# One hybrid layer on one core: preloaded banks 0 to 2, copies out inside the last step, and pauses ahead of transposes

## The chip, the cores and the metric

The kernel runs on one core of one Trainium2 chip. The metric is the device time of one execution in microseconds (us). TensorE (PE) multiplies, VectorE (DVE), ScalarE (ACT) and GpSimd (POOL) work on tiles, SyncE (SP) issues most of the transfers.

## The reference: what is computed

One layer over 256 latent tokens `x` and 256 context tokens `ctx` of width 4096, in float32. A modulation is computed from two vectors, normalised rows are scaled and shifted by it, projected by a 4096 x 13312 matrix, mixed in three ways, and projected back:

```python
mod_l = silu(c) @ w_ada + b_ada          # 4096 -> 3 * 4096, the same for c_ctx
hl = rmsnorm(xl, norm_g) * (1.0 + sc_l) + sh_l
hc = rmsnorm(xc, norm_g) * (1.0 + sc_c) + sh_c
z_l, z_c = hl @ w_in, hc @ w_in          # split into conv (3), recurrence (2), attention q k v and gate (4)
ya = conformer_conv(...)                 # GLU, depthwise conv over 31, LayerNorm, pointwise
yb = sum of two RG-LRU scans, started from the context's last state
yc = 8x16 neighbourhood attention over the latent grid, plus attention to the context
mix = concat(ya * silu(a_gate), yb * silu(r_gate), yc * silu(c_gate))
out = rmsnorm(xl + g_l * (mix @ w_out), final_g)
```

Only the latent stream is returned, so of the context's projections only r_x, k and v are needed.

## The kernel before

**Phases.** Weights are float32 and every product is made of three: a weight tile is split into a high part `hi` (ACT, L411) and a low part `lo` (DVE, L417), the activations likewise, and PE multiplies hi by hi, hi by low, low by hi (L426, all inside `Step.products`). A *chunk* is 512 columns of a weight matrix. In the first phase both token streams are multiplied by the columns for r, k and v, in 10 chunks of `w_in`: r0, k0, v0, k1, v1, k2, v2, k3, r1, v3 (`kinds`, L861). An r or k chunk ("both") fills 4 PSUM banks of 128 x 512, a v chunk ("tm") 2. The second phase does the remaining columns for the latent tokens alone, with the mixers' work on the other engines, and ends with `w_out`.

**Blocks.** The 32 row tiles of `w_in` come in 13 blocks of 1, 1, 2, 2, 2 and then 3 rows (`BLOCKS`), because the modulation for a row has to be there before its activations h can be made. So each of the 10 chunks is visited 13 times, and its sums live in SBUF tiles `acc` between the visits. At the start of a visit some banks are *preloaded* with the sums so far (ACT copy, L859) and the matmuls add to them; at its end the bank is copied back out (*spilled*, ACT copy, L848). A bank that isn't preloaded starts at zero, and DVE adds it to `acc` (L853). Before the change banks 1, 2, 3 of an r or k chunk and bank 1 of a v chunk are preloaded (`ch.pre`, L875). `spill` and `preload` of all banks are called one after the other at the end of a chunk's last step (L1232 to L1237). The banks of the chunks come from a pool of five (tag "g", L80); three more serve everything else (tag "aux", counted by `take` and `give`).

**Steps and order.** A step is up to two rows of a chunk, so a block of three rows has steps of two and one, and the last step of a chunk is its tail. The program order is written out by the generator: `do_step` emits, in rounds of three products (one bank, one row), the products of a step, and between rounds the work of threads (`run_threads`). A thread is a Python generator; `yield None` waits for the next round. Threads of rank 0 (the end of a modulation, the making of h) go ahead at every round, others only while the planner's budget for DVE and ACT allows. `ahead.split_high()` and `split_low()` in a step make the parts for the step after next; `load_until` issues transfers four steps ahead into six buffers.

**Modulation.** `MODS` lists groups of rows with a flag: part 0 (scale) is always multiplied on PE (`mod_matmuls`, L268, into a bank `psa`), part 1 (shift) on PE or, with flag 1, on DVE (L921, L923, into the tile `gboth`). `spread` deals the pieces over the steps so that each group is done by its due time, which lies half the preceding block's planned time ahead of the block that uses it (L892). The end of a group is a thread: `mod_finish` copies `psa` to SBUF (DVE, L273), transposes it on PE (L280), sums (DVE, L283) and adds (L260, L262); `mod_finish_vector` transposes `gboth` (L297) for each of two streams and sums (L299). Then `next_h` makes h (DVE L362, ACT L363, DVE L370), and a block's first chunk calls `drain` on it, which runs the thread to its end.

**Recurrence.** From the last block on, two threads run `recurrence` for eight heads each, with two matmuls per head (L533, L534).

Of the kernel before, what the change touches and what calls it, by code (L numbers as in the profile page):

```python
# [17 lines left out]
P = 128  # L18
# [7 lines left out]

BLOCKS = [1, 1, 2, 2, 2, 3, 3, 3, 3, 3, 3, 3, 3]

MODS = [(1, 1, 0), (2, 2, 0), (4, 2, 0), (6, 2, 0), (8, 4, 0), (12, 4, 0), (16, 4, 1), (20, 4, 1), (24, 4, 1),
        (28, 4, 1)]  # L30

NPG, NWD, NRAW, NHI = 69, 6, 6, 3
# [11 lines left out]
def tile_hybrid_layer(ctx: ExitStack, tc: tile.TileContext, x, c, cctx_tok, c_ctx, w_ada, b_ada,  # L44
# [89 lines left out]
    def drain(*ths):  # L134

        for _ in range(2000):
            if all(t.done for t in ths):
                return
            for t in list(threads):
                if not t.done and (t in ths or t.rank == 0 or clock["aux"] > 0):  # L140
                    advance(t, True)
            clock["tick"] += 1
        raise RuntimeError("a thread waits for ever")

    def take(n):

# [7 lines left out]
    with tc.manual_schedule():  # L154
# [116 lines left out]
        def mod_finish(part, k0, s, ps):  # L271

            V.tensor_copy(adas[:, :s * P], ps[:, :s * P])  # L273
            give(1)
            yield 0.6 * s / 4 + .1, 0
            yield None
            yield from take(1)
            pm = bank("psm")
            for i in range(s):
                tr(pm[:, i * P:(i + 1) * P], adas[:, i * P:(i + 1) * P], ident)  # L280
            yield None
            sums = small(8, "sums").rearrange("p (k o) -> p k o", o=2)
            V.reduce_sum(sums[:, :s], pm[:, :s * P].rearrange("p (k q o) -> p k o q", q=4, o=32)[:, :, 0:2], axis=AX.X)  # L283
            mod_columns(part, k0, s, sums)
            give(1)
            yield 0.5, 0

        def mod_finish_vector(k0, s):
            sums = small(8, "sums").rearrange("p (k o) -> p k o", o=2)
            yield None  # L290
            yield None
            for b in range(2):
                yield None
                yield from take(1)
                pm = bank("psm")
                for i in range(s):
                    tr(pm[:, i * P:(i + 1) * P], gboth[:, b, i * P:(i + 1) * P], ident)  # L297
                yield None
                V.reduce_sum(sums[:, :s, b:b + 1], pm[:, :s * P].rearrange("p (k n) -> p k n", n=P), axis=AX.X)  # L299
                give(1)  # L300
                yield 0.7, 0
            mod_columns(1, k0, s, sums)
            yield 0.2, 0
# [78 lines left out]
        acc = {}  # L382
# [115 lines left out]
        def recurrence(d):  # L498
# [12 lines left out]
            for n in range(8):  # L511
                while n > rec_done[1 - d] + 1:
                    yield None
                Xr = acc[("r", n // 4), n % 4]
                x3 = Xr.rearrange("p (s t) -> p s t", s=2)
                gw = rec[2 + n % 2][:, d]
                G.dma_start(gw[:, 0], w_r[0, d, n])
                G.dma_start(gw[:, 1], w_i[0, d, n])
                ci = 8 * d + n
                A.activation(xc, Xr, AF.Identity, scale=tap(3 if d == 0 else 0), bias=col("rcb", ci))  # L520
                yield 0, 0.7
                yield None
                for s in (1, 2, 3):
                    if d == 0:
                        o, i_, w = xc3[:, :, s:], x3[:, :, :T - s], tap(3 - s)
                    else:
                        o, i_, w = xc3[:, :, :T - s], x3[:, :, s:], tap(s)
                    V.scalar_tensor_tensor(o, i_, w, o, ALU.mult, ALU.add)
                    yield 0.75, 0
                yield None  # L530
                yield from take(2)
                pr, pi = bank("pr"), bank("pi")
                mm(pr, gw[:, 0], xc, start=True, stop=True)  # L533
                mm(pi, gw[:, 1], xc, start=True, stop=True)  # L534
                yield None
                yield None
                A.activation(ti, pi, AF.Tanh, bias=hbi[:, ci:ci + 1], scale=0.5)
                give(1)

                A.activation(e, pr, AF.Relu, bias=nbr[:, ci:ci + 1], scale=-1.0)  # L540
                yield 0, 1.4
                A.activation(pr, pr, AF.Tanh, bias=hbr[:, ci:ci + 1], scale=0.5)
                A.activation(e, e, AF.Exp, scale=-1.0)
                yield 0, 1.4
                A.activation(pr, pr, AF.Abs)
                yield 0, 0.6
                yield None
                V.scalar_tensor_tensor(ti, ti, 1.0, xc, ALU.add, ALU.mult)
                V.scalar_tensor_tensor(e, pr, 1.0, e, ALU.add, ALU.mult)
                yield 1.4, 0  # L550
                yield None
                A.activation(xc, e, AF.Exp, scale=n4[:, ci:ci + 1])
                A.activation(e, e, AF.Tanh, scale=p4[:, ci:ci + 1])
                yield 0, 1.4
                A.activation(pr, xc, AF.Square)
                yield 0, 0.6
                yield None
                V.scalar_tensor_tensor(e, pr, 1.0, e, ALU.add, ALU.mult)
                give(1)
                yield 0.7, 0  # L560
                yield None
                A.activation(e, e, AF.Sqrt, bias=tiny)
                yield 0, 3.2
                yield None
                V.scalar_tensor_tensor(ti, e, 0.5, ti, ALU.mult, ALU.mult)
                yield 0.7, 0
                if d == 0:
                    V.tensor_tensor_scan(e[:, :T], xc[:, :T], ti[:, :T], 0.0, ALU.mult, ALU.add)
                    V.tensor_tensor_scan(hold[:, n % 2], xc[:, T:], ti[:, T:], e[:, T - 1:T], ALU.mult, ALU.add)
                    yield 1.5, 0  # L570
                else:
                    for s, init in ((0, 0.0), (1, e[:, 0:1])):
                        sl = slice(s * T, s * T + T)
                        V.tensor_tensor_scan(e[:, sl][:, ::-1], xc[:, sl][:, ::-1], ti[:, sl][:, ::-1], init,
                                             ALU.mult, ALU.add)
                    yield 1.5, 0
                    while rec_done[0] <= n:
                        yield None
                    V.tensor_add(ybs(n), hold[:, n % 2], e[:, T:])
                    yield 0.4, 0  # L580
                rec_done[d] += 1
# [259 lines left out]
            unpair(sil)  # L841


        def spill(ch, key):

            for i, b in enumerate(ch.banks):
                if i in ch.pre:
                    A.copy(acc[key, i], b)  # L848
                elif (key, i) not in acc:
                    acc[key, i] = page([P, 512], name="acc")  # L850
                    (A.copy if i % 2 else V.tensor_copy)(acc[key, i], b)
                else:
                    V.tensor_add(acc[key, i], acc[key, i], b)  # L853

        def preload(ch, key):
            for i in range(ch.nb):
                ch.banks[i] = bank("g" + ch.kind, "g")
                if i in ch.pre:
                    A.copy(ch.banks[i], acc[key, i])  # L859

        kinds = [("r", 0), ("k", 0), ("v", 0), ("k", 1), ("v", 1), ("k", 2), ("v", 2), ("k", 3), ("r", 1), ("v", 3)]  # L861
        starts = [sum(BLOCKS[:i]) for i in range(len(BLOCKS))]
# [1 line left out]
        begin = {}  # L864
        t = 0.0
        for bi, s in enumerate(BLOCKS):
# [3 lines left out]
            for ci, key in enumerate(order):  # L870
# [1 line left out]
                c0 = {"r": C_RX, "k": C_K, "v": C_V}[kind] + 512 * i  # L872
                ch = Chunk(key, win, ks, c0, "tm" if kind == "v" else "both", ctx_ops if kind == "v" else None)
                if bi:
                    ch.pre = {1} if kind == "v" else {1, 2, 3}  # L875
                    ch.before = lambda ch=ch, key=key: preload(ch, key)
                ch.after = lambda ch=ch, key=key: spill(ch, key)
                ch.block, ch.place = bi, ci
                for st in ch.steps():
                    st.at = t  # L880
# [5 lines left out]
        class Mod:  # L886
            def __init__(self, part, k0, s, vec):
# [1 line left out]
                self.thread = None  # L889
                self.held = []  # L890
                bi = max(i for i in range(len(BLOCKS)) if starts[i] <= k0)
                self.due = begin[bi] - (0.5 * (begin[bi] - begin[bi - 1]))  # L892
                self.n = 2 if s > 2 else 8 // s

            def items(self):
# [293 lines left out]
        def do_step(i):  # L1189
# [23 lines left out]
            if tail:  # L1213
                clock["v"] -= PAGE * (ch.nb - len(ch.pre))
                clock["a"] -= PAGE * (1.7 * len(ch.pre) if ch.block else 1)
            if ahead:
                ahead.split_high()
            work = st.mods + st.vecs
            n = len(st.kp)
            for p in range(ch.nb * n):  # L1220
# [8 lines left out]
                clock["tick"] += 1  # L1229
                if p == n - 1 and ahead:  # L1230
                    ahead.split_low()
            if tail:  # L1232
                if ch.after is not None:
                    ch.after()
                nxt = steps[i + 1].ch if i + 1 < len(steps) else None
                if nxt is not None and nxt.before is not None:
                    nxt.before()  # L1237
                if ch.block == len(BLOCKS) - 1 and ch.place == 1:
                    rec_threads.extend(spawn(recurrence(d), 2) for d in range(2))
            if ch in chunks3 and i + 1 < len(steps) and head:  # L1240
# [92 lines left out]
```

## Time and profile before

| | |
|---|---|
| median of 3 runs | 2430.76 us (2427.84 to 2431.7) |
| the profiled execution | 2434.84 us |
| its span, first to last instruction | 2433.1 us |
| PE, DVE, ACT busy | 95%, 66%, 52% of the span |
| read from HBM | 544.58 MB |

PE is 0.9 busy or more in most of the 40 slices of the page; the first phase takes the first 1008 us. A matmul's end is modelled, so a busy PE is not always multiplying at its full rate, and the distance of two starts tells more than the duration.

### The profile page before, as it was taken

The page shows a single profiled execution, that of the slowest core. Times are in us where ns is not written, and L with a number is a line of the kernel's source. Part 1 is how long each engine was busy: PE and PEld are TensorE (multiplying, and loading weights), DVE is VectorE, ACT ScalarE, POOL GpSimd, SP SyncE. Part 2 cuts the span into 40 slices and gives each one's busy share as a digit, 9 for nine tenths or more (in the row PEclk, how much of TensorE's full clock was granted, in tenths as well). Part 3 has the DMA queues.
Part 4 walks back from the last instruction along what each step waited for, and adds up shares of the span by engine and source line. Part 5 has one row for each costly group of instructions (what it writes and reads, how often), then busy time and mean ns, then how long its engine had stood idle before and what let it go on. Part 6 is the DMA issues. An engine that isn't in the chain of part 4 may idle for free.

```text
span 2433.1 us, 29898 instructions
## 1 busy us (share of the span) xinstructions
PE 2301.2 (95%) x10761; PEld 1753.7 (72%) x10761; DVE 1594.2 (66%) x2196; ACT 1271.5 (52%) x1860; POOL 96.0 (4%) x133
## 2 busy tenths in 40 slices
PE   6999889899989999999999999999999999999997
PEld 4555556676666776777768888788888778888886
DVE  4543446676766543667667798788967677667655
ACT  4665444455545666777776444444444444444433
POOL 0000000000000000000100100110011021000000
PEclk8999999999999999999999999999999999999999
DMA  9988788767767543555557888878878678887864
GB/s 278 288 262 265 270 273 290 246 220 239 259 208 246 182 121 91 157 157 169 159 162 222 228 280 263 202 242 260 261 204 231 189 217 293 266 265 251 262 213 164
DMA packets 293484, 550.76 MB, mean 226 GB/s; under 512 B 19199, under 2 KB 60887, under 8 KB 293335
## 3 DMA queue, kind: packets, MB, share of 16 engines
q1 hardware_dynamic: 287904, 536.94, 68.5%
q0 software_dynamic: 4480, 11.54, 4.2%
q8 instruction: 84, 1.38, 0.2%
q14 instruction: 65, 0.53, 0.1%
q10 hardware_dynamic: 951, 0.37, 0.1%
HBM read 544.58 MB, written 4.19 MB: 226 GB/s over the span
## 4 chain that ended last, share of the span: by engine, by line
PE 71%; ACT 3%; DVE 3%; issue 2%; DMA 1%; POOL 0%; SPq 0%; ACTq 0%; DVEq 0%; POOLq 0%
PE gtm L426 50%; PE gboth L426 13%; PE y L682 1%; ACT hi L411 1%; PE sc L642 1%; DMA raw<-in_w_in_dram 1%; PE gcm L426 1%; PE psa L268 1%; ACT acc L848 1%; DVE lo L417 1%; PE pr L533 1%; PE pi L534 1%; PE pt L667 1%; PE turn L602 0%; DVE gboth L923 0%
## 5 line engine op out<-in xcount | busy, mean ns | idle before, releaser
L417 DVE TENSOR_TENSOR lo<-raw,hi 128x1024 fp32r<-128x1024 f32 (+1 forms) x660 | 756.7, 1149 | 624.9 <-ACT hi L411 596.5
L411 ACT CAST hi<-raw 128x1024 fp32r<-128x1024 f32 (+1 forms) x660 | 648.5, 986 | 725.5 <-PE gtm L426 420.9
L426 PE MATMUL gtm<-hi,lh 128*128 128x512 f32 x2560 | 835.6, 401 | 1.0 <-ACT hi L411 1.0
L426 PEld LDWEIGHTS gtm<-hi,lh 128*128 128x128 f32 x2560 | 482.6, 189 | 112.0 <-issue 11.2
L426 PE MATMUL gboth<-h,hi 128*128 128x512 f32 x1536 | 505.8, 411 | 47.8 <-ACT acc L848 43.0
L426 PE MATMUL gtm<-lo,lh 128*128 128x512 f32 x1280 | 501.5, 392 | 7.2 <-DVE lo L417 7.2
L426 PEld LDWEIGHTS gboth<-h,hi 128*128 128x128 f32 x1536 | 281.6, 192 | 179.5 <-ACT acc L848 69.4
L426 PE MATMUL gboth<-h,lo 128*128 128x512 f32 x768 | 305.4, 398 | 0.0
L426 PE MATMUL gtm<-hi,mix 128*128 128x512 f32 x976 | 304.0, 391 | 0.0
L426 PEld LDWEIGHTS gtm<-lo,lh 128*128 128x128 f32 x1280 | 241.6, 189 | 69.3 <-DVE lo L417 11.4
L426 PEld LDWEIGHTS gtm<-hi,mix 128*128 128x128 f32 x976 | 183.7, 188 | 37.8
L426 PE MATMUL gtm<-lo,mix 128*128 128x512 f32 x488 | 190.4, 390 | 0.2 <-DVE lo L417 0.2
L848 ACT COPY acc<-gboth 128x512 f32<-128x512 f32 x216 | 125.0, 586 | 123.3 <-PE gboth L426 113.0
L426 PE MATMUL gtm<-hi,h 128*128 128x512 f32 x512 | 182.6, 408 | 3.9 <-DVE acc L853 2.2
L426 PEld LDWEIGHTS gboth<-h,lo 128*128 128x128 f32 x768 | 147.4, 192 | 34.0 <-DVE lo L417 0.3
L923 DVE SCALAR_TENSOR_TENSOR gboth<-raw,scol,gboth 128x512 f32<-128x512 f32 x248 | 169.6, 747 | 0.0
L1123 DVE SCALAR_TENSOR_TENSOR gboth<-raw,scol,gboth 128x1024 f32<-128x1024 f32 x124 | 160.1, 1292 | 0.0
L426 PEld LDWEIGHTS gtm<-hi,h 128*128 128x128 f32 x512 | 96.8, 189 | 54.7 <-issue 22.1
L859 ACT COPY gboth<-acc 128x512 f32<-128x512 f32 x216 | 117.6, 594 | 0.0
L268 PE MATMUL psa<-raw,cpad 128*32 128x512 f32 (+2 forms) x1152 | 112.6, 469 | 1.1 <-DMA raw<-in_w_ada_dram 0.6
L426 PEld LDWEIGHTS gtm<-lo,mix 128*128 128x128 f32 x488 | 91.9, 188 | 19.6 <-DVE lo L417 0.8
L426 PE MATMUL gtm<-lo,h 128*128 128x512 f32 x256 | 101.0, 395 | 0.1
(228 smaller groups left out, 1650.1 us busy)
## 6 DMA issues: line engine op xcount, KB each, us to landing
raw<-in_w_in_dram SPq DMA_DIRECT2D x430, 512.0 KB, 4.4
raw<-in_w_ada_dram SPq DMA_DIRECT2D x384, 512.0 KB, 4.7
raw<-in_w_out_dram SPq DMA_DIRECT2D x128, 512.0 KB, 4.6
raw<-in_w_in_dram SPq DMA_DIRECT2D x100, 256.0 KB, 4.2
xp<-in_ctx_dram SPq DMA_DIRECT2D x16, 256.0 KB, 6.9
xp<-in_x_dram SPq DMA_DIRECT2D x16, 256.0 KB, 6.6
xr<-in_x_dram POOLq DMA_DIRECT2D x16, 256.0 KB, 4.6
raw<-in_w_pw_dram SPq DMA_DIRECT2D x8, 512.0 KB, 7.7
```

The costliest lines, as they stand in the source:

```text
L268: mm(ps[32 * q:32 * q + 32, :W], cpad[(k + j) // 16][:, (k + j) % 16, :], raw[:, j, :], start=(k + j < 4), stop=(k + j >= KT - 4))
L411: A.copy(self.hi[:, :n], self.raw[:, :n])
L417: V.tensor_sub(self.lo[:, :n], self.raw[:, :n], self.hi[:, :n].bitcast(F32))
L426: one = lambda o, l, r, start, stop: mm(o, l, r, start=start, stop=stop, skip_group_check=True)
L533: mm(pr, gw[:, 0], xc, start=True, stop=True)
L534: mm(pi, gw[:, 1], xc, start=True, stop=True)
L642: mm(ps, q[i][:, qt * P:(qt + 1) * P], acc[("k", g), i], start=True, stop=True)
L667: tr(ps[:, kt * T + qt * P:kt * T + qt * P + P], Ps[0][qt][:, (2 * kp + kt) * P:(2 * kp + kt + 1) * P], ident)
L848: A.copy(acc[key, i], b)
L859: A.copy(ch.banks[i], acc[key, i])
L923: V.scalar_tensor_tensor(a, self.raw[:, j], s, a, ALU.mult, ALU.add)
L1123: V.scalar_tensor_tensor(a, self.raw, s, a, ALU.mult, ALU.add)
```

## The change

Five things. Banks 0, 1 and 2 (0 of a v chunk) are preloaded instead of 1, 2, 3 (1). The preloads of the next chunk are emitted ahead of the tail's products (bank 0, and bank 1 too where the chunk is a v) and behind each bank's copy out, and each bank is copied out right behind its last products. Pauses of six rounds stand ahead of the transposes of modulation sums, and of two rounds ahead of the recurrence's matmuls; the vector form makes both streams' transposes in one round. The shift of rows 12 to 15 goes to DVE, that of 16 to 19 to PE. The due time lies at most 25 us ahead of its block.

```diff
-MODS = [(1, 1, 0), (2, 2, 0), (4, 2, 0), (6, 2, 0), (8, 4, 0), (12, 4, 0), (16, 4, 1), (20, 4, 1), (24, 4, 1),
+MODS = [(1, 1, 0), (2, 2, 0), (4, 2, 0), (6, 2, 0), (8, 4, 0), (12, 4, 1), (16, 4, 0), (20, 4, 1), (24, 4, 1),
         (28, 4, 1)]
...
+    def pause(n):
+        for _ in range(n):
+            yield None
...
# mod_finish, between the copy to SBUF and the transposes
-            yield None
+            yield from pause(6)
             yield from take(1)
             pm = bank("psm")
...
# mod_finish_vector
-            yield None
-            yield None
+            yield from pause(6)
+            pms = []
             for b in range(2):
-                yield None
                 yield from take(1)
                 pm = bank("psm")
                 for i in range(s):
                     tr(pm[:, i * P:(i + 1) * P], gboth[:, b, i * P:(i + 1) * P], ident)
-                yield None
+                pms.append(pm)
+            yield None
+            for b, pm in enumerate(pms):
                 V.reduce_sum(sums[:, :s, b:b + 1], pm[:, :s * P].rearrange("p (k n) -> p k n", n=P), axis=AX.X)
...
# recurrence, ahead of the two matmuls
-                yield None
+                yield from pause(2)
                 yield from take(2)
...
-        def spill(ch, key):
-
-            for i, b in enumerate(ch.banks):
-                if i in ch.pre:
-                    A.copy(acc[key, i], b)
-                elif (key, i) not in acc:
-                    acc[key, i] = page([P, 512], name="acc")
-                    (A.copy if i % 2 else V.tensor_copy)(acc[key, i], b)
-                else:
-                    V.tensor_add(acc[key, i], acc[key, i], b)
-
-        def preload(ch, key):
-            for i in range(ch.nb):
+        def spill(ch, i):
+
+            key, b = ch.name, ch.banks[i]
+            if i in ch.pre:
+                A.copy(acc[key, i], b)
+            elif (key, i) not in acc:
+                acc[key, i] = page([P, 512], name="acc")
+                (A.copy if i % 2 else V.tensor_copy)(acc[key, i], b)
+            else:
+                V.tensor_add(acc[key, i], acc[key, i], b)
+
+        def preload(ch, i):
+            if i < ch.nb and i in ch.pre and ch.banks[i] is None:
                 ch.banks[i] = bank("g" + ch.kind, "g")
-                if i in ch.pre:
-                    A.copy(ch.banks[i], acc[key, i])
+                A.copy(ch.banks[i], acc[ch.name, i])
...
                 if bi:
-                    ch.pre = {1} if kind == "v" else {1, 2, 3}
-                    ch.before = lambda ch=ch, key=key: preload(ch, key)
-                ch.after = lambda ch=ch, key=key: spill(ch, key)
+                    ch.pre = {0} if kind == "v" else {0, 1, 2}
...
-                self.due = begin[bi] - (0.5 * (begin[bi] - begin[bi - 1]))
+                self.due = begin[bi] - min(25.0, 0.5 * (begin[bi] - begin[bi - 1]))
...
# do_step, ahead of ahead.split_high()
+            nxt = steps[i + 1].ch if tail and i + 1 < len(steps) else None
+            spilled = tail and ch.block is not None
+            if spilled:
+                for b in range(1 if ch.nb == 4 else 2):
+                    preload(nxt, b)
...
# do_step, at the end of each round
+                if spilled and j == n - 1:
+                    spill(ch, b)
+                    preload(nxt, b + (1 if ch.nb == 4 else 2))
             if tail:
                 if ch.after is not None:
                     ch.after()
-                nxt = steps[i + 1].ch if i + 1 < len(steps) else None
-                if nxt is not None and nxt.before is not None:
-                    nxt.before()
```

## Rows read from the trace of the kernel before

**Rows 1.** The page's first part: busy us, share of the span, instructions.

```profile
PE 2301.2 (95%) x10761; PEld 1753.7 (72%) x10761; DVE 1594.2 (66%) x2196; ACT 1271.5 (52%) x1860; POOL 96.0 (4%) x133
```

**Rows 2.** Stretches at the ends of blocks: busy us, granted clock, DMA share, GB/s.

```profile
52.00:130.00 78.00, 73.26 (x503) 42.01 (x503) 38.73 (x76) 48.42 (x90) 0.00 (x0) 0.96 0.88 278
...
339.00:441.00 102.00, 90.33 (x407) 58.24 (x405) 60.42 (x95) 44.23 (x75) 0.00 (x0) 0.95 0.81 271
...
612.00:692.00 80.00, 75.56 (x345) 54.49 (x344) 57.82 (x87) 43.87 (x74) 0.00 (x0) 1.00 0.75 244
...
854.00:925.00 71.00, 67.98 (x289) 53.24 (x289) 29.62 (x42) 44.00 (x74) 2.12 (x4) 1.00 0.38 115
```

**Rows 3.** Timeline, one chunk's end: start us, us, instruction, [idle before <-releaser].

```profile
439.73 0.39 PE L426 MATMUL gtm<-lo,h 128*128 128x512 f32 x1
...
439.96 0.39 PE L426 MATMUL gtm<-hi,h 128*128 128x512 f32 x1
440.44 0.59 ACT L848 COPY acc<-gtm 128x512 f32<-128x512 f32 x1 [0.79 <-PE gtm L426]
...
441.08 0.73 PE L426 MATMUL gboth<-h,hi 128*128 128x512 f32 x2 [0.73 <-ACT acc L848]
...
441.65 0.40 PE L426 MATMUL gboth<-h,lo 128*128 128x512 f32 x1
```

**Rows 4.** The same stretches, instructions of L268 alone: PE, PEld, clock, DMA, GB/s.

```profile
339.00:441.00 102.00, 15.10 (x104) 2.31 (x104) 0.95 0.81 271
```

**Rows 5.** PE's waits from 52 to 1008: us in total, times, longest us.

```profile
PE gboth L426 <- ACT acc L848: 43.0, 46, 5.6
PE psm L280 <- DVE adas L273: 11.9, 5, 5.0
PE psm L297 <- DVE gboth L923: 5.6, 3, 3.0
```

**Rows 6.** Stretches at half clock, and one at full clock; columns as in rows 2.

```profile
137.00:140.40 3.40, 3.40 (x16) 1.93 (x14) 0.50 (x3) 0.78 (x2) 0.00 (x0) 0.50 0.69 211
294.00:304.20 10.20, 7.07 (x18) 5.31 (x19) 9.65 (x22) 5.40 (x11) 0.00 (x0) 0.50 0.52 174
...
707.00:713.80 6.80, 6.03 (x14) 4.77 (x15) 5.25 (x10) 3.70 (x7) 0.00 (x0) 0.50 0.12 18
...
528.00:692.00 164.00, 152.21 (x693) 109.57 (x693) 116.94 (x178) 88.07 (x147) 0.00 (x0) 1.00 0.75 244
```

**Rows 7.** Timeline around two long waits of PE, at 707.8 and at 486.0.

```profile
703.75 2.46 DVE L362 SCALAR_TENSOR_TENSOR xp<-xp,modG,R 128x256 f32<-128x256 f32 x6
...
704.27 2.50 ACT L363 ACTIVATE h<-xp,modS 128x256 fp32r<-128x256 f32 x6 [6.21 <-DVE xp L362]
...
707.77 1.22 PE L426 MATMUL gboth<-h,hi 128*128 128x512 f32 x2 [5.60 <-ACT acc L848]
...
486.03 1.22 PE L426 MATMUL gboth<-h,hi 128*128 128x512 f32 x2 [4.83 <-ACT acc L848]
```

**Rows 8.** Timeline around the longest wait ahead of transposes.

```profile
346.93 0.68 DVE L273 COPY adas<-psa 128x512 f32<-128x512 f32 x1
...
347.67 1.12 PE L280 MATMUL psm<-ident,adas 128*128 128x128 f32 x4 [5.00 <-DVE adas L273]
```

**Rows 9.** PE's waits from 528 to 692.

```profile
PE gboth L426 <- ACT acc L848: 8.8, 12, 0.7
```

**Rows 10.** ACT's waits from 266 to 441.

```profile
ACT hi L411 <- DMA raw<-in_w_in_dram: 47.0, 15, 6.0
```

**Rows 11.** A stretch of the first phase; columns as in rows 2.

```profile
283.50:293.80 10.30, 7.11 (x34) 3.59 (x34) 5.27 (x7) 3.43 (x6) 0.00 (x0) 1.00 0.93 325
```

**Rows 12.** PE's waits from 52 to 441.

```profile
PE gboth L426 <- ACT acc L848: 11.1, 14, 1.4
...
PE psm L297 <- DVE gboth L923: 1.9, 1, 1.9
```

**Rows 13.** PE's waits over the whole span.

```profile
PE pr L533 <- issue: 10.7, 6, 2.6
```

## What the change should do to the time: the prediction, worked out ahead of the run

> **What bounds the kernel now.** The first part of the page [rows 1] shows TensorE (PE) busy for 2301.2 of 2433.1 us, VectorE (DVE) 1594.2, ScalarE (ACT) 1271.5: PE sets the end. Then look at the change's stretch alone, the first phase, cut near the ends of its blocks [rows 2]. The block at 854 to 925 loads no modulation and shows the price of three rows of `w_in`: 71 us, of which 3 x 96 products at 0.2285 us (the distance of two neighbouring starts, 439.73 and 439.96, is 0.23 [rows 3]) are 65.8. Earlier blocks are longer, since modulation matmuls share PE (104 in one block [rows 4]), and since PE waits. The view of waits says for whom [rows 5]: 43.0 us in 46 waits for ACT's copy at L848 (a bank of sums copied out), 11.9 in 5 for the DVE copy ahead of the transposes at L280, 5.6 in 3 for the DVE sums ahead of the transposes at L297. That is 60 of the phase's 956 us, with more behind it: after a longer wait PE runs at half its clock for a while [rows 6].
>
> **The change part by part.** All durations are from the profiled execution: 2434.84 us, with a span of 2433.1; that is 4.1 above the median of the runs shown (2430.76).
>
> *A, chunk ends.* [Rows 3] show one. PE's last product of a chunk starts at 439.96; ACT copies its bank out from 440.44 to 441.03, and PE starts the next chunk at 441.08, 0.05 us after that copy, though the next bank needs no preload and the pool has five. I read from it that banks are handed out in the order in which they came free: the three preloads, which stand ahead in the program, took the free ones, and PE's bank 0, which asks last, got the one that was just being emptied. After the change banks 0 (and 1) of the next chunk are asked for at the start of the last step and filled while PE still multiplies; only the bank that starts fresh (3, or 1 of a v chunk) asks late, several products after the chunk's beginning. The number of copies stays (3 out and 3 in per r or k chunk, 1 and 1 per v chunk, some 0.59 us each [rows 3]; one bank is added by DVE as before), so ACT has the same work, spread earlier. Two of the 46 waits (5.60 us at 707.8, 4.83 at 486.0 [rows 7]) have another cause, C. The other 44 are 32.6 us, 0.74 each. A wait costs more than its idle time: the last matmul's 0.39 us no longer overlaps the next start (0.39 - 0.23 = 0.16), and the first one behind it takes 0.34 instead of 0.23 (441.08 to 441.65 for two). So 44 x (0.74 + 0.16 + 0.11) = 44.5 us. Bounds: 0, if the wait only moves to another bank, and 44.5. I take nine tenths, **40**: a v chunk's last step is as short as 6 x 0.2285 = 1.4 us on PE, its two early preloads (1.2 us) just fit, and where ACT is already late they don't.
>
> *B, pauses ahead of transposes.* The 8 waits are 17.5 us, with 0.27 each 19.7. `pause(6)` puts 5 more rounds of three products (5 x 0.685 = 3.4 us) between DVE's copy and the transposes at L280, and 3 more (2.1 us) at L297. The wait of 5.00 us in [rows 8] shrinks to 1.6; the longest at L297, 3.0 [rows 5], to 0.9; the others vanish. Left 2.5, gained **17** (bounds 0 and 19.7). Behind the later transposes only the same thread is queued; the vector form now holds two of three auxiliary banks for a round, which nothing in the phase waits for.
>
> *C, ACT held by the making of h.* In [rows 7] ACT stands for 6.21 us before the activation at L363, for DVE, which is late with the columns of the modulation; the chunk's copies stand behind it, and PE is idle 5.60 us. The wait at 486 is of the same kind. Columns, and h behind them, now come 3.4 us of products later, so DVE can catch up, and a preloaded bank or two covers 1.4 to 2.7 us of PE. Of 10.4 + 0.5 us I take **7** as gained; bounds 0 and 10.9.
>
> *D, the clock.* Six stretches, from the one at 137.0 to the one at 707.0 [rows 6], were granted 0.50, that is 1.2 of 2.4 GHz: 37.3 us together, in which PE was busy for 30.1, so 15.0 us were lost. Each follows a wait of B or C of 1.9 us or more. Three quarters should come back with these: **11** (bounds 0 and 15). A wait of 0.7 us does not cost the clock here: from 528 to 692 there are 12 of A's waits [rows 9] at a granted clock of 1.00 [rows 6]. The Trainium skill, "TensorE: Matmul & The Clock Gate", section "A second HAM failure mode: psum-queue depth-cycling", says otherwise: small idles between groups of matmuls that cycle through PSUM banks make the clock swing between its levels. By that rule the whole 15 would hang on A and come back with it, 4 us more than I count; the trace disagrees, with 1.00 in that stretch.
>
> *Given back to the transfers.* Up to 441 us the DMA engines are 0.81 to 0.88 busy [rows 2], and from 266 on ACT waits 47.0 us for weights [rows 10]; a stretch of ten us reaches 0.93 and 325 GB/s [rows 11]. Of the gains, 14 of A's waits (11.1 us [rows 12], by the reckoning above 0.9 x (11.1 + 14 x 0.27) = 13.4), 13.8 of B (11.9 and 1.9 [rows 5, 12], with 6 x 0.27, less 1.6 that stay) and 6.8 of D (four of the six stretches) lie there: 34 us of 389. Keeping them all, the same bytes would need a share of about 0.92. Against that, the swap in `MODS` (rows 12 to 15 now on DVE, 16 to 19 on PE, the number of each unchanged) and the later due times move loads out of the block at 339 to 441, the one with 104 modulation matmuls [rows 4]. I take half back: **-17** (bounds -34 and 0). The swap itself I cost at nothing: PE and DVE get the same instructions at another time, beside 60 us of DVE work in the 102 of that block [rows 2]; without that cover a late split of weights would show as a wait of PE for L417, of which [rows 5] have none.
>
> *New.* In the two blocks of one row the modulation is due half a block (10.9 us, 16 rounds) ahead of its use. Pause, transposes and sums (7 rounds), h (2) and some 2.5 us of their execution (4) now take 13 of them, so PE may wait up to 3 us at each of the next two heads: **-2** (-6 to 0). The extra round in the recurrence (16 times 0.685 us) stands in a chain whose result is used hundreds of us later; PE's waits at its matmuls, 10.7 us [rows 13], may shrink by some: 0 (-3 to +5).
>
> Sum: 40 + 17 + 7 + 11 - 17 - 2 = **56 us**. 2434.84 - 56 = 2379, as a median 4.1 less: **2375 us**. Behind the phase the work is unchanged and PE the bound, so the time carries through.
>
> **The rivals.**
> 1. *The early blocks are bound by transfers.* For it: [rows 10, 11]. Then all 34 goes back: 75 - 34 - 2 = 39, 2392 us. Against: PE's time in these blocks is accounted for by products, modulation and the waits named.
> 2. *The wait moves to the fresh bank.* Bank 1 of a v chunk is asked for by its first product; if it gets the bank that DVE's addition empties last, A's wait returns at 48 such places (4 v chunks in 12 blocks), 1.0 us each. Then A falls away, and of B, C and D's 35 some 10 go back and 2 are new: 23 remain, 2408 us. Against: by the order of asking in [rows 3] that product gets the bank that is free longest.
> 3. *Slower: h comes late at every block.* Finishing 5 rounds later, and due 25 instead of half a block (32.7 us in the planner's time) ahead, the columns miss the block's head; the program then drains the thread with no products between. By [rows 6, 7] one such miss costs 5.6 us of idle time and 3.0 by the half clock, 8.6; at 12 heads 103. B, C and D then gain nothing, A 40: 2434.84 + 63 - 4.1 = 2494 us. It turns slower from 5 heads on (5 x 8.6 = 43). Against: 25 us are 36 rounds, and 13 are needed.
> 4. *No change:* ACT's copies now wait inside the tail, and delay the splits of weights by as much as is gained. Against: ACT is busy 44 of 80 to 102 us of a block [rows 2], and its last copy now ends before the chunk does.
>
> **How the numbers follow.** Forecast (gains of 45 to 76, 2355 to 2386): 0.60. Rival 1: 0.15. Rival 2: 0.10. Slower, by rival 3 or a part of it: 0.08. Rival 4: 0.04. The rest, 0.03, is a partial gain of 6 to 20 us. The range 2350 to 2412 holds the forecast and the first two rivals. About 0.2% (5 us) is what a measurement of this kernel can tell from no change. Faster: 0.60 + 0.15 + 0.10 + 0.03 = 0.88; same 0.04; slower 0.08.
>
> **What would show it.** In the changed trace: PE's waits for ACT's copy out down from 43.0 to under 8 us; those ahead of the two kinds of transposes from 17.5 to under 5; fewer than three half-clock stretches in the phase; the block that ended at 925 at 67 instead of 71 us. The forecast is wrong if the waits go but the blocks before 441 stay as long (rival 1), if PE waits at bank 1 of v chunks (rival 2), or if PE stands at the heads of blocks for h (rival 3).

## The result, and the profile after

The changed kernel takes 2352.84 us (median of 4 runs, 2350.91 to 2354.04) against 2430.48 of the kernel before in the same comparison: a ratio (time after by time before) of 0.9681, 95% interval 0.9664 to 0.9698, that is 77.6 us less. The forecast was 2375 us, 56 less, in a range of 2350 to 2412. The gain lies just outside the 45 to 76 us that stood for the forecast itself, and inside the range, close to its lower end. Direction and place held; the chunk ends gave more than forecast, the pauses less, and the recurrence's round, forecast at nothing, gave some 8 us. In a second comparison on another chip, where the kernel before takes 2424.88 us, the ratio was 0.9701 (0.9679 to 0.9723). Below, 0.969, the mean of the two, stands for the changed kernel where another is set beside it; 0.001 is 2.4 us. The one trace of the kernel before is of an execution of 2434.84 us, 4 us above the median here and 8 to 11 above the medians of the kernel before beside the experiments (2424.16 to 2427.11), so what two traces differ by overstates the gain by as much.

Lines of the changed kernel: the copy out is L853 (L848 before), DVE's addition L858 (L853), the preload L863 (L859), the transposes L284 and L300 (L280, L297), products L431 (L426), the recurrence's matmuls L538 (L533). The page's first part:

```profile
PE 2265.3 (96%) x10761; PEld 1747.4 (74%) x10761; DVE 1597.0 (68%) x2196; ACT 1268.7 (54%) x1860; POOL 93.8 (4%) x133
```

Every engine has the same number of instructions as in [rows 1]; 83 us of span are gone. The stretches that answer to [rows 2], with the whole first phase last (columns as there):

```profile
52.00:130.00 78.00, 72.82 (x499) 42.91 (x498) 39.55 (x76) 49.49 (x93) 0.00 (x0) 0.94 0.89 282
328.00:421.00 93.00, 85.59 (x396) 56.42 (x395) 63.74 (x99) 43.15 (x73) 0.00 (x0) 0.96 0.84 286
576.00:650.00 74.00, 73.93 (x345) 55.29 (x344) 55.06 (x82) 44.78 (x74) 0.00 (x0) 1.00 0.80 266
795.00:861.00 66.00, 66.00 (x293) 54.66 (x292) 30.95 (x43) 44.44 (x75) 2.12 (x4) 1.00 0.44 127
52.00:935.00 883.00, 854.78 (x4199) 603.47 (x4199) 544.18 (x856) 525.06 (x881) 7.62 (x14) 0.99 0.76 246
```

The phase lasts 883 instead of 956 us. The block without modulation went from 71 to 66 us, the price of its products alone; the one at 612 to 692 from 80 to 74. By 421 us (441 before) some 21 us are won, by the phase's end 74. PE's waits in the phase, beside [rows 5]:

```profile
PE gtm L431 <- DVE acc L858: 9.1, 3, 6.9
PE gboth L431 <- ACT acc L853: 5.6, 4, 3.7
PE gboth L431 <- ACT gboth L863: 5.1, 1, 5.1
...
PE psm L300 <- DVE gboth L925: 1.8, 1, 1.8
PE psa L272 <- DMA raw<-in_w_ada_dram: 1.6, 2, 1.1
PE gtm L431 <- ACT acc L853: 1.4, 2, 0.7
```

46 waits for the copy out have become 4 (and 2 in v chunks, where there was 1), and 17.5 us ahead of transposes 1.8. The end of a v chunk, to set beside [rows 3], from ACT's timeline, and then from PE's:

```profile
594.37 1.11 ACT L863 COPY gboth<-acc 128x512 f32<-128x512 f32 x2
...
596.97 0.59 ACT L853 COPY acc<-gtm 128x512 f32<-128x512 f32 x1
597.45 0.60 ACT L863 COPY gboth<-acc 128x512 f32<-128x512 f32 x1
```

```profile
597.23 0.39 PE L431 MATMUL gtm<-hi,h 128*128 128x512 f32 x1
597.45 0.61 PE L431 MATMUL gboth<-h,hi 128*128 128x512 f32 x2
```

Two banks were filled at 594.4 to 595.5, and PE goes from chunk to chunk in 0.22 us, where it took 1.12 before. The stretches at half clock, three in the phase beside the six of [rows 6], and one at full clock (not counted are one that ends at 58 us in both kernels, and one of 3.4 us at 949 in the kernel before, behind a wait of the recurrence's matmuls, which is gone):

```profile
299.90:306.60 6.70, 3.53 (x8) 2.81 (x9) 4.90 (x10) 4.64 (x9) 0.00 (x0) 0.50 0.30 93
388.60:395.30 6.70, 4.22 (x13) 1.71 (x14) 6.18 (x14) 5.93 (x12) 0.00 (x0) 0.50 0.47 120
122.40:125.70 3.30, 3.30 (x14) 1.91 (x14) 1.42 (x2) 1.94 (x4) 0.00 (x0) 0.50 0.26 70
501.00:650.00 149.00, 148.93 (x698) 111.22 (x700) 112.94 (x171) 89.06 (x148) 0.00 (x0) 1.00 0.79 261
```

### The profile page after: what moved, and what is told of

Read it like the earlier page. It is cut to its first block, busy times and chain, and to the rows that moved or that the text cites. A ratio compares the mean times of both kernels' runs of the same rounds, so it can differ in the third digit from the quotient of the medians.

```text
span 2350.1 us, 29790 instructions
## 1 busy us (share of the span) xinstructions
PE 2265.3 (96%) x10761; PEld 1747.4 (74%) x10761; DVE 1597.0 (68%) x2196; ACT 1268.7 (54%) x1860; POOL 93.8 (4%) x133
## 4 chain that ended last, share of the span: by engine, by line
PE 84%; DMA 5%; DVE 5%; ACT 3%; issue 2%; ACTq 0%; POOL 0%; SPq 0%; DVEq 0%; POOLq 0%
PE gtm L431 52%; PE gboth L431 21%; PE psa L272 4%; DMA raw<-in_w_in_dram 2%; DVE lo L422 2%; ACT hi L416 1%; PE y L687 1%; PE sc L647 1%; PE gcm L431 1%; PE pr L538 1%; DMA xp<-in_ctx_dram 1%; DMA raw<-in_w_ada_dram 1%; PE pi L539 1%; DVE gboth L925 1%; PE pt L672 1%
## 5 line engine op out<-in xcount | busy, mean ns | idle before, releaser
L431 PE MATMUL gtm<-hi,lh 128*128 128x512 f32 x2560 | 833.8, 400 | 0.7 <-ACT hi L416 0.7
L431 PEld LDWEIGHTS gtm<-hi,lh 128*128 128x128 f32 x2560 | 482.1, 188 | 111.0 <-issue 10.8
L431 PE MATMUL gtm<-lo,lh 128*128 128x512 f32 x1280 | 501.4, 392 | 8.0 <-DVE lo L422 8.0
L431 PE MATMUL gboth<-h,hi 128*128 128x512 f32 x1536 | 491.3, 401 | 12.5 <-ACT acc L853 5.6
L431 PEld LDWEIGHTS gboth<-h,hi 128*128 128x128 f32 x1536 | 281.6, 189 | 130.1 <-issue 58.5
L431 PE MATMUL gtm<-hi,mix 128*128 128x512 f32 x976 | 303.9, 391 | 0.0
L431 PE MATMUL gboth<-h,lo 128*128 128x512 f32 x768 | 302.0, 393 | 0.1
L431 PEld LDWEIGHTS gtm<-lo,lh 128*128 128x128 f32 x1280 | 241.3, 188 | 70.4 <-DVE lo L422 13.2
L431 PEld LDWEIGHTS gtm<-hi,mix 128*128 128x128 f32 x976 | 183.7, 188 | 37.8
L431 PE MATMUL gtm<-lo,mix 128*128 128x512 f32 x488 | 190.3, 390 | 0.2 <-DVE lo L422 0.2
L431 PE MATMUL gtm<-hi,h 128*128 128x512 f32 x512 | 177.6, 400 | 10.6 <-DVE acc L858 9.1
L431 PEld LDWEIGHTS gboth<-h,lo 128*128 128x128 f32 x768 | 145.2, 189 | 34.2 <-DVE lo L422 2.5
L853 ACT COPY acc<-gboth 128x512 f32<-128x512 f32 x216 | 124.8, 586 | 59.6 <-PE gboth L431 55.9
L431 PEld LDWEIGHTS gtm<-hi,h 128*128 128x128 f32 x512 | 96.7, 189 | 45.7 <-DVE acc L858 12.2
L863 ACT COPY gboth<-acc 128x512 f32<-128x512 f32 x216 | 124.0, 593 | 5.8 <-DVE acc L858 2.6
L431 PEld LDWEIGHTS gtm<-lo,mix 128*128 128x128 f32 x488 | 91.9, 188 | 19.7 <-DVE lo L422 0.8
L858 DVE TENSOR_TENSOR acc<-acc,gboth 128x512 f32<-128x512 f32 x72 | 49.4, 686 | 77.8 <-PE gboth L431 77.8
```

Source lines behind the costliest of these rows:

```text
L431: one = lambda o, l, r, start, stop: mm(o, l, r, start=start, stop=stop, skip_group_check=True)
L863: A.copy(ch.banks[i], acc[ch.name, i])
```

## The experiments

Each was timed against the kernel before; the diffs are against the changed kernel unless said otherwise.

**The chunk ends alone.** MODS, due times, both modulation threads and the recurrence are those of before; only the set of preloaded banks and the places of copies and preloads are changed.

> Only the chunk ends are changed (banks 0 to 2 preloaded, early preloads, each bank copied out behind its last products); pauses, MODS, due times and the recurrence as before. Theory 1 (the gain is a sum of separate terms): the 44 short waits for the copy out go, 40 to 45 us, and the waits ahead of transposes (about 17 us) and at least four half-clock stretches stay: 2385 to 2391 us. Rival (the chunk ends are the one cause: with sums preloaded early, ACT's lateness no longer reaches PE, and the clock comes back by itself): 2360 us or less, one half-clock stretch or none.

Measured: 2372.86 against 2424.71 us, ratio 0.9783 (0.9768 to 0.9797), 52 us. PE's waits in its first phase (its lines are one lower than the changed kernel's, L430 for L431):

```profile
PE psm L284 <- DVE adas L277: 12.6, 6, 4.1
PE psm L301 <- DVE gboth L924: 8.6, 4, 4.4
PE gboth L430 <- ACT gboth L862: 4.3, 1, 4.3
...
PE gboth L430 <- ACT acc L852: 2.6, 2, 2.1
```

The short waits are gone, those ahead of transposes stay and are even longer (21.2 for 17.5 us). So it is not the one cause, but it is more than the 40 to 45 us expected, and lies between the two expectations: besides the 44 short waits, the longer of the waits of C went (one of 4.3 us is left), and the half-clock stretches shrank from 41 us (the six, and the one at 949) to 24, seven of 3.4.

**The pauses of the modulation alone**, put into the kernel before (the vector form's two transposes in one round come with them, as in the change; cut short):

```diff
-            yield None
+            yield from pause(6)
...
```

> Only the two pauses of the modulation's ends are added to the kernel before (six rounds ahead of both kinds of transposes); chunk ends as before. Theory 1: terms B, C and D, 17 + 7 + 11 = 35 us: 2395 us, with some 44 waits of 0.7 us for the copy out left and the clock full but for two stretches or fewer, although PE idles 0.7 us at nearly every chunk end. Rival (chunk ends are the one cause): 2420 us or more. By the rule that short idles between bank groups make the clock swing, the half-clock stretches would stay at six or so.

Measured: 2408.89 against 2424.71 us, ratio 0.9930 (0.9915 to 0.9945), 16 us: between the two expectations, half of the 35. (The spans of the two traces differ by 27; see the remark on the trace of the kernel before.) PE's waits in the first phase, then those from 500 to 690, then the row of that stretch:

```profile
PE gboth L431 <- ACT acc L853: 34.4, 44, 1.8
PE gtm L431 <- ACT acc L853: 9.7, 4, 3.8
...
PE psm L284 <- DVE adas L277: 0.5, 1, 0.5
```

```profile
PE gboth L431 <- ACT acc L853: 9.5, 13, 0.7
```

```profile
500.00:690.00 190.00, 177.88 (x812) 128.83 (x811) 140.53 (x219) 104.04 (x174) 0.00 (x0) 1.00 0.75 245
```

The waits ahead of transposes go (B), and of the six half-clock stretches three of 3.4 us are left, 10 of 37 us (D). But the two long waits of C only gave way to others, at v chunks: 9.7 us in 4 waits, which was 1.6 in one. ACT still stands before the activations for h, with the copies behind it, as here (ACT, then PE):

```profile
686.18 2.51 ACT L368 ACTIVATE h<-xp,modS 128x256 fp32r<-128x256 f32 x6 [4.84 <-DVE xp L367]
```

```profile
689.73 0.50 PE L431 MATMUL gtm<-hi,h 128*128 128x512 f32 x1 [2.57 <-ACT acc L853]
```

And 13 waits of 0.7 us in 190 us leave the clock at 1.00 (it falls at 690.1, behind the wait of 2.57). The swing that the Trainium skill ("TensorE: Matmul & The Clock Gate", "A second HAM failure mode: psum-queue depth-cycling") names does not come at this size of idle.

**Without the recurrence's second round.**

```diff
-                yield from pause(2)
+                yield None
                 yield from take(2)
```

> The changed kernel with one round instead of two ahead of the recurrence's matmuls. Theory 1 as predicted: the extra round is worth 0 (-3 to +5), so 2350 to 2357 us. Rival: the 7 us that the changed kernel gained between 955 and 1290 us, behind the first phase, come from this round: 2359 to 2361 us, with PE's waits at the recurrence's matmuls back near 17 us from 11.

Measured: 2358.74 us, ratio 0.9723 (0.9709 to 0.9738), 8 us behind 0.969: the rival was right. The stretch of the recurrence is 274 us long in the changed kernel; without the round it is 281, as it was before (1009 to 1290). The changed kernel's row of the windows, and PE's largest wait in that stretch:

```profile
935.00:1209.00 274.00, 259.78 (x1069) 199.99 (x1068) 190.34 (x221) 206.10 (x257) 13.31 (x22) 0.99 0.57 167
```

```profile
PE pr L538 <- issue: 6.7, 5, 1.9
```

The same of the kernel without the round:

```profile
939.00:1220.00 281.00, 263.47 (x1064) 201.78 (x1063) 190.48 (x222) 205.30 (x256) 13.54 (x22) 0.96 0.56 162
```

```profile
PE pr L538 <- issue: 10.1, 5, 2.6
```

The waits themselves differ by 3.4 us. The rest goes with the granted clock, 0.96 of 281 us against 0.99 of 274, but how much of that is the round's is open: the next run has the round and the same 6.7 us of waits, and its stretch (938 to 1216) took 278 us at 0.97. By the two intervals the 8 us are known to some 5 either way.

**With MODS and due times as before.**

```diff
-MODS = [..., (12, 4, 1), (16, 4, 0), ...]
+MODS = [..., (12, 4, 0), (16, 4, 1), ...]
-                self.due = begin[bi] - min(25.0, 0.5 * (begin[bi] - begin[bi - 1]))
+                self.due = begin[bi] - (0.5 * (begin[bi] - begin[bi - 1]))
```

> The changed kernel with MODS and the due times as before. Theory 1: the swap and the due times are worth nothing on PE, 2350 to 2357 us. Rival: they took loads out of the block that lasted from 339 to 441 us, and that is where 10 us of the gain arose: 2362 us or more, with that block near 103 us again instead of 93.

Measured: 2354.86 us, ratio 0.9701 (0.9683 to 0.9719), which cannot be told from the changed kernel. As predicted, worth nothing that can be measured, given the pauses. The block that the rival names takes 95 us (325 to 420), 93 in the changed kernel and 102 before, so most of what it gained does not come from the swap.

**The changed kernel without the modulation's pauses** (the diff of the second experiment, reversed):

> The changed kernel without the two pauses ahead of the transposes of modulation sums (the recurrence's second round, MODS, due times and chunk ends stay changed). By the sum of the prediction they are worth B, C and D, 35 us less some 10 given back: ratio 0.979. By the runs so far (all of the change less the ends alone, less the recurrence's round, less MODS and due times) about 10 us: ratio 0.972 to 0.975, with PE's waits ahead of the transposes back at 15 us or more. Rival (with sums preloaded early the waits ahead of transposes only displace others): ratio 0.968 to 0.970.

Measured: 2358.0 us, ratio 0.9705 (0.968 to 0.9731). The interval holds the rival and the lower part of the 10 us. PE's waits in its phase (lines one lower again):

```profile
PE gtm L430 <- ACT acc L852: 7.1, 3, 3.9
PE psm L301 <- DVE gboth L924: 4.6, 2, 3.9
PE gboth L430 <- DVE lo L421: 3.8, 3, 1.4
```

No wait at the transposes of L284 has come back, although the pause ahead of them is gone: with the ends changed, and within these intervals, either the pauses or the swap and the due times will do. Both together are worth some 15 us (5 either way): that is the distance of the ends alone (0.9783) from everything but the recurrence's round (0.9723).

**One preload fewer**, in the kernel before, all at the chunk's end:

```diff
-                    ch.pre = {1} if kind == "v" else {1, 2, 3}
+                    ch.pre = {1} if kind == "v" else {2, 3}
```

> The kernel before with one preload less: r and k chunks preload banks 2 and 3 only, bank 1 starts fresh and is added by DVE like bank 0 (72 additions of 0.68 us more on DVE, 144 copies of 0.59 us less on ACT); everything still at the chunk's end. Theory (banks are handed out in the order in which they came free, and bank 0 got the last one because three preloads asked ahead of it): with two ahead of it, bank 0 of a chunk behind a v chunk gets a bank that is long free, the waits for the copy out fall from 46 to some 10, and 25 to 36 us go: ratio 0.985 to 0.990. Rival (PE waits because ACT is late with its copies in general): some 46 waits stay, and the time changes by under 8 us.

Measured: 2400.44 against 2424.88 us, ratio 0.9897 (0.9880 to 0.9914), 24 us, although DVE does 72 additions more. PE's largest wait:

```profile
PE gboth L426 <- ACT acc L848: 14.9, 11, 5.1
```

11 waits for 46. In the kernel before 37 of the 46 stand at a chunk's first product behind a v chunk, of 48 such places; here none does, and 9 of the 11 left are at an r or k chunk behind another. A v chunk has one copy out in either kernel, so it is not that ACT has fewer copies ahead of PE; it is the order in which banks are handed out, with three preloads asking ahead of bank 0. (In the code `preload` calls `bank` for bank 0 first, in both kernels; what counts, by this run, is the first instruction that uses the bank, and for bank 0 that is PE's product.)

**All preloads behind the tail**, copies out still inside it:

```diff
-            if spilled:
-                for b in range(1 if ch.nb == 4 else 2):
-                    preload(nxt, b)
...
-                    preload(nxt, b + (1 if ch.nb == 4 else 2))
+            if spilled:
+                for b in range(4):
+                    preload(nxt, b)
```

> The changed kernel with all preloads behind the tail's last products, as before; the copies out stay inside the tail and banks 0, 1, 2 are the preloaded ones. Theory (what counts is that the next chunk's first bank is filled while PE still multiplies): bank 0's preload now starts when the tail ends, so PE waits some 0.7 us or more at each of the 120 ends, at L861's successor for the preload, 85 to 130 us more than the changed kernel: slower than the kernel before, ratio 1.00 to 1.02. Rival (the copies' place inside the tail carries the gain): a ratio of 0.98 or less.

Measured: 2426.21 against 2424.16 us, ratio 1.0012 (0.9999 to 1.0025), some 77 us behind the changed kernel. PE waits for the preloads:

```profile
PE gboth L431 <- ACT gboth L863: 43.6, 50, 7.2
PE gtm L431 <- ACT gtm L863: 30.5, 37, 6.3
```

So with this set of banks the copies' place gives nothing by itself; the filling of the next chunk's first bank while PE multiplies does. The size is a little under the 85 to 130 us expected, since PE waits at 87 of the 120 ends.

**The old set of banks in the new order.**

```diff
-                    ch.pre = {0} if kind == "v" else {0, 1, 2}
+                    ch.pre = {1} if kind == "v" else {1, 2, 3}
...
-                    preload(nxt, b)
+                    preload(nxt, b + 1)
...
-                    preload(nxt, b + (1 if ch.nb == 4 else 2))
+                    preload(nxt, b + (2 if ch.nb == 4 else 3))
```

> The changed kernel with the old set of preloaded banks (1, 2, 3, and 1 of a v chunk), each preload as early as before its move in the changed kernel (so bank 0 starts fresh and is asked for by PE's first product). Theory (bank order): two preloads ask ahead of bank 0 behind a v chunk, one behind others, so bank 0 finds one that is long free or was emptied early in the tail; no preload stands between PE and its first bank: the changed kernel's time, ratio 0.966 to 0.972. Rival (the set is the operative part, since the fresh bank must be the last): short waits for the copy out or for DVE's addition come back at some 50 or more ends, ratio 0.98 or more.

Measured: 2454.21 us, ratio 1.0116 (1.0100 to 1.0133): slower than before. The waits of PE, then one of ACT's, both in the first phase:

```profile
PE gboth L431 <- ACT acc L853: 75.5, 61, 8.6
PE gboth L431 <- DVE acc L858: 16.8, 9, 3.1
```

```profile
ACT gboth L863 <- DVE acc L858: 44.7, 24, 5.0
```

My expectation had miscounted: bank 3 is asked for behind the first copy out, so three preloads still ask ahead of bank 0, and the short waits stay. New is that early preloads now ask for the bank that DVE is still adding from, 24 times, and ACT, which works in order, stands with everything behind it. (Nearly all of these stand at an r or k chunk with another behind it, two in each of 12 blocks.) That the bank emptied by DVE is the last one is thus part of what makes the change work.

**The making of h four rounds later.**

```diff
             while not mods_done(ks):
                 yield None
+            if bi > 2:
+                yield from pause(4)
             yield from make_h(ks)
```

> The changed kernel; from block 3 on the making of h starts four rounds after its modulation is done, so that ACT's activations for h stand later in ACT's queue than DVE's columns need. Theory (what is left of PE's long waits before 441 us, 6.94 us at 303 and 5.10 at 391 with a half-clock stretch of 6.8 us behind each, is ACT or DVE held by the making of h): both waits and their stretches go, 12 + 6 us at most, so 10 to 18 us less than the changed kernel, a ratio to the kernel before of 0.961 to 0.964. Rival (late transfers are the cause and would show elsewhere): the changed kernel's 0.968, with as much waiting at other places. Rival on the other side: h comes late at block heads, ratio over 0.97.

Measured: 2348.6 us, ratio 0.9683 (0.9657 to 0.9709): the rival. The waits of 6.94 and 5.10 us became 1.8 and none, but as much waiting came at other places:

```profile
PE gboth L431 <- ACT acc L853: 7.4, 5, 3.9
PE gboth L431 <- ACT gboth L863: 4.1, 2, 2.4
PE gtm L431 <- DVE acc L858: 3.9, 3, 1.8
PE gtm L431 <- ACT acc L853: 3.4, 2, 2.8
```

**Fewer bytes.**

```diff
+                if not m.vec and self.k // m.n % 2:
+                    self.raw = m.last
+                    return
...
+                m.last = self.raw
```

> The changed kernel with half of the modulation's weights for PE left unread (each such tile is used for two groups of rows, so the modulation is another one); every instruction on PE, ACT and DVE stays. In the blocks before 421 us this takes some 26 to 34 MB of about 113 away. Theory (what the changed kernel still loses there, 23 us of PE's waits and some 10 us by the half clock behind them, comes from transfers that are late): block ends before 421 us come 15 to 30 us earlier, and the whole is 2320 to 2335 us, ratio 0.957 to 0.963. Rival (those waits come from DVE and ACT alone): under 5 us, ratio 0.967 to 0.971.

Measured: 2330.21 us, ratio 0.9610 (0.9596 to 0.9624), some 20 us less than the changed kernel. The block that ended at 421 ends 16 us earlier, the next one 19.5, and no more is gained behind it. Four blocks of the changed kernel, their row of the windows and ACT's waits for weights:

```profile
130.00:421.00 291.00, 271.57 (x1380) 172.39 (x1380) 162.49 (x277) 153.23 (x257) 0.00 (x0) 0.98 0.84 279
```

```profile
ACT hi L416 <- DMA raw<-in_w_in_dram: 72.5, 28, 6.5
```

The same blocks with fewer bytes:

```profile
130.00:405.00 275.00, 264.42 (x1368) 170.28 (x1366) 162.22 (x274) 154.66 (x255) 0.00 (x0) 0.99 0.66 209
```

```profile
ACT hi L416 <- DMA raw<-in_w_in_dram: 2.9, 1, 2.9
```

Late transfers cost the changed kernel 16 us up to 421 and some 4 behind it. But of PE's 19.4 us of waits in these four blocks 10.7 are left, two of them long, 4.6 us at 294 and 4.7 at 376: the counterparts of those at 303 and 391 stay, so the theory holds in part only. Whether by their bytes or by the buffers that they hold stays open, since fewer transfers also hold fewer buffers.

**More bytes** (100 transfers of 256 KB on POOL's queue into a page that nothing reads) failed as a test:

> The changed kernel with 100 more transfers of 256 KB (26 MB, of w_out into a tile that nothing reads) on the POOL queue in blocks 1 to 5, about 5 per cent of the phase's time ahead of 421 us. Theory as predicted (those blocks are half bound by transfers): at 300 GB/s the bytes are 87 us of transfer, half of it shows, 30 to 50 us more than the changed kernel. Rival 1 of the prediction (wholly bound): 70 to 90 us more. Rival (not bound, the transfers are late only because buffers come free late): under 10 us more, the DMA share of these blocks up from 0.83 to over 0.95.

Measured: 2645.46 us, ratio 1.0898 (1.0868 to 1.0928). The page is handed on to a tile of sums, whose first copy then waited for all 100 transfers:

```profile
403.43 1.07 ACT L853 COPY acc<-gboth 128x512 f32<-128x512 f32 x2 [293.94 <-DMA junk<-in_w_out_dram]
```

Behind that one stall the blocks are as long as in the changed kernel, and hold no extra bytes. It says nothing on the question, which the run with fewer bytes answers in part. (The changed kernel run again beside these, 2351.14 us, is the second ratio named at the top:)

> The changed kernel itself, on the chip of the others, as their common measure: ratio 0.968 to the kernel before.

## Why the prediction was right, point by point

*A, chunk ends: right in mechanism, too small.* Predicted 40, less the 7 that are its share of what is given back: 33. The ends alone measured 52. The 44 short waits all went, which at the prediction's own price is its upper bound, 44.5 us; ACT's lateness in short tails, for which I took a tenth off, did not show. The rest was booked elsewhere: one of the two waits of C and 17 us of half clock went too, which I counted with the pauses (C, and part of D). The reading of [rows 3], that banks go out in the order in which they come free and bank 0 asked last, is shown by the run with one preload fewer. Rival 2 is there in small: three waits, 9.1 us, of v chunks for DVE's addition; the longest, at 303.07, in the timelines of DVE and of PE. Here DVE is late with the addition because the making of h stands ahead of it:

```profile
299.95 2.46 DVE L375 SCALAR_TENSOR_TENSOR h<-xp,modS,h 128x256 fp32r<-128x256 f32 x6
302.33 0.68 DVE L858 TENSOR_TENSOR acc<-acc,gboth 128x512 f32<-128x512 f32 x1
```

```profile
303.07 0.80 PE L431 MATMUL gtm<-hi,h 128*128 128x512 f32 x1 [6.94 <-DVE acc L858]
```

*B, C, D: too large.* Predicted 35, net of what is given back 25. Pauses, swap and due times together measured 15 on top of the ends, the pauses alone in the kernel before 16. B went as subtracted (17.5 to 1.8 us), and D, in the run with the pauses alone, as well: three quarters of the half-clock stretches went. The step that failed is C, "DVE can catch up": in that run the waits of 10.4 us gave way to 9.7 at v chunks, with ACT still standing 4.84 us before the activations for h. In the changed kernel the two longest waits left stand behind the making of h as well: the one at 303 above, and one at 391 (ACT, then PE, below). Making h four rounds later only moved the idle time elsewhere.

```profile
388.04 2.50 ACT L368 ACTIVATE h<-xp,modS 128x256 fp32r<-128x256 f32 x6 [3.97 <-DVE xp L367]
```

```profile
391.08 1.22 PE L431 MATMUL gboth<-h,hi 128*128 128x512 f32 x2 [5.10 <-ACT gboth L863]
```

*Given back: of the right size, but not isolated.* 17 us were predicted for the blocks before 441; the run with fewer bytes shows 16. But these 16 are all that late transfers cost the changed kernel there, not what the change gave back: ACT waited for weights before it too, 52.5 us in 20 waits from 52 to 441, against 75.7 in 31 from 52 to 421 after. The kernel before was not run with fewer bytes, so the share of the change is open, and that 16 lies beside 17 is in part luck.

*The swap and the due times: right* at nothing, in the presence of the pauses.

*The recurrence's round: wrong.* I gave it 0 (-3 to +5); it is worth some 8 us, 3.4 of them waits. I saw its wait of 10.7 us on PE's path [rows 13] and put what goes of it at nothing, and did not count the clock at all; how much of the clock's part is the round's stays open.

*New waits at the heads of the one-row blocks: none seen.* PE's only wait for h in the phase is one of 1.8 us, there before too. Rival 3 did not occur.

*The signs named:* waits for the copy out under 8 us (5.6 and 1.4: met), ahead of transposes under 5 (1.8: met), the block at 67 us (66: met), fewer than three half-clock stretches (three: missed; each lies at a long wait at 121, 303 or 391 us).

In sum 52 + 15 + 8 = 75 us, with ratios 0.9783, 0.9723 and 0.969 one behind the other, against 77.6 measured. That the forecast of 56 came as near as it did is in part luck: the ends were 19 us too low and the round 8, the pauses 10 too high. Of the 83 us by which the spans of the two traces differ 74 arise in the first phase and 7 in the recurrence's stretch; the last 2 arise behind it and were not looked into.

## What to carry to other kernels

Where a pool of banks turns round, look at who asks for a bank first: the instruction that PE runs next should not ask behind preloads that are needed later, and the bank that another engine empties last should be needed last. An engine that works in order hands its wait on to everything behind it, so look at what stands ahead of a copy or a preload in its engine's program (here the activations for h, for which ACT stood up to 6.21 us). And count a wait of PE with the clock that it may cost: behind most idle times of 2 us and more the granted share was 0.5 for 3 to 10 us (not behind each: one of 2.96 us at 561 in the kernel before left it at 1.00), behind single ones of 0.7 us it was not.

## What the runs showed that I had not expected

Early preloads into the wrong banks are worse than late ones into the right banks: the old set in the new order is some 25 us slower than all preloads behind the tail (ratios 1.0116 and 1.0012). Transfers that write the same tile on POOL's queue ran one behind another: 98 of 256 KB with a median of 3.0 us from issue to landing, some 80 GB/s in the stretch where nothing else ran.
